# A gate stage with rows turned on VectorE, h added by accumulating loads and finished a pair later, and one row ring of four buffers

## The chip, the cores and the metric

The kernel runs on one core of a Trainium2 chip. The metric is the device time of one execution in microseconds (us), lower is better. The core has a matrix engine (TensorE, PE in the profile, with a separate row PEld for the loading of its weights), VectorE (DVE), ScalarE (ACT), GpSimd (POOL) and SyncE (SP). Each runs its own instructions in order; they wait for each other by semaphores. Transfers between the chip's memory (DRAM) and the on-chip buffers (SBUF) are issued by SP, ACT and POOL, each into a queue of its own, and run beside the engines. Matrix products go to banks of PSUM, which VectorE and ScalarE read.

## What is computed

One layer of a streaming encoder over 2048 prompt rows and 32 sample rows of width 1024, cut to what matters here:

```python
hn = rmsnorm(h, g_mix)
proj = hn @ w_in                                  # input projection, then two mixers -> yA, yB
h = h + concat([yA, yB], axis=-1) @ w_out         # "output stage"
gate = sigmoid(rmsnorm(h, g_ple) @ w_ple_gate)
h = h + (p @ w_ple) * gate                        # "embedding" p @ w_ple, then "gate stage"
y = rmsnorm(h, g_final)
```

Everything is float32; each operand of a product is split into a high and a low part, and three products (high-high, high-low, low-high) are added up.

## The kernel before, in words

**Tiles.** The 2048 rows are 16 tiles of 128, and the sample rows are a seventeenth tile of 32. From the output stage on, the tiles are taken in pairs (0 and 1, 2 and 3, ...). A pair is a 256x1024 by 1024x1024 product, which `seven` makes in seven products of quarters (Strassen-Winograd) in place of eight. With A11, A12 the upper tile's and A21, A22 the lower tile's halves, the kernel forms S1 = A21 + A22, S2 = S1 - A11, S3 = A11 - A21 and S4 = A12 - S2 on VectorE, and splits all of them; T1 to T4 are such sums of the weights. One quarter product is 12 matmuls of 128x128 by 128x512. They go to three banks X, Y, Z: X takes A11 W11, then adds S2 T2, then S3 T3, then A22 T4; between two of these, the state of X is read out by `carry` (parts kept for later: c_00, c_01 from X and c_11 from Z) or by `out` (a finished quarter). The next product into a bank therefore waits until the read before it is done. The order within a pair is X (A11 W11), Z (S1 T1), X (S2 T2), X (S3 T3), Y (A12 W21), Z (S4 W22), X (A22 T4); the tile scheduler orders instructions of neighbouring steps on each engine by what it reckons to be ready. A dictionary `between` gives work to be put at steps 1 to 6 between the products.

**Output stage** (about 559 to 722 us). `seven` runs for pairs o0 to o14, and the sample follows o12 (`ol`). x, the tile's input rows (128x1024), is loaded by `load_rows` on SP from a ring `xh` of 3 buffers. `h_ops` adds x to the products on VectorE: in `carry`, c_00 and c_01 read the first tile's x and c_11 the second's; in `out`, the finished h is written over x. `done_h` squares and sums the row on ScalarE (`sumsq`) and stores h to DRAM (`h_d`) on SP. `prep_h` loads the next pair's activations y on SP (ring `ya` of 5) and forms its sums. Beside this, one block of 128 gate weights per pair (two in places) is scaled: `scale_gate(k)` loads it on POOL's queue as two halves of 128x512 (gs) from a ring of its own, `qa`; after the next pair ScalarE scales both and stores them to `g_d` on its own queue. `next_gate` starts the scaling of the block before and the load of the next.

**Embedding** (722 to 762 us): p @ w_ple is made for most tiles and stored in `e_d`.

**Gate stage** (762 to 940 us): the sample goes first (`plain`), then pairs 0 to 12 in a loop, then `last_pair` (tiles 14 and 15). `prep_g(i + 2)` runs between the products of pair i and brings h of the next pair back from DRAM with the channel in the partition. For the pair's second tile, `turned_here` loads the rows in four blocks on SP and turns 32x32 blocks on VectorE. For the first tile, `turned` loads the rows (hn), ScalarE copies them in two halves (ho, in `qa`), and TensorE turns them by four transposes each into PSUM (pth). For the result, e and h of both tiles are loaded again on SP (`e` in `ya`, `h` in `xh`). `gate_ops` takes a quarter of the product: ScalarE applies the sigmoid, VectorE multiplies e by it and adds that to h. `done_g` then squares the row on ScalarE (`sumsq`, whose small root runs on POOL), multiplies by the root and g_final on VectorE, and stores the row on POOL's queue.

**What sets the order.** SP's transfers are issued in program order, and each waits for its buffer to come free, so one that waits holds up those behind it. POOL's queue carries the gate weights (output stage) and the finished rows (gate stage); ScalarE's queue carries the scaled gate weights. Buffers in a ring are handed out in turn, and a new user of a buffer waits for the last reader or writer of the former one.

Lines of the kernel before that matter: pools 1102, `h_ops` 1116 (VectorE's operations show as L1120), `done_h` 1143 (store at L1146), `scale_gate` 1162 (load L1170, scale L1174, store L1175), `load_rows` 324 (L327), the load of y at L314, `turned` with copy L1280 and transposes L1282, `turned_here` with L1293, `gate_ops` with L1310 to L1314, `done_g` L1318 (L1321, store L1322), `last_pair` with L1371 to L1401, and the products at L167.

Of the kernel before, what the change touches and what calls it, by code (L numbers as in the profile page):

```python
# [9 lines left out]
F32 = mybir.dt.float32  # L10
F32R = mybir.dt.float32r
AF = mybir.ActivationFunctionType
ALU = mybir.AluOpType
# [21 lines left out]
def trunk(ctx, tc, x_p, x_s, c_conv, c_pool, p_p, p_s, g_mix, w_in, conv_w, conv_b, pool_w,  # L35
# [271 lines left out]
    def ring4(t, name):  # L307
        return t.tile([P, D], F32, tag="t", name=name)
# [791 lines left out]

    with ExitStack() as s2:
        pool = lambda name, bufs: s2.enter_context(tc.tile_pool(name=name, bufs=bufs, reuse_waits="tile"))
        w3, qa, xh, st, ss, cmb = (pool(*a) for a in (
            ("w3", 1), ("qa", 2), ("xh", 3), ("st", 4), ("ss", 3), ("cmb", 8)))

        def quarters(name, W):
            c = halves(slot(f"{name}_c"))
# [54 lines left out]
        def scale_gate(k):  # L1162

            ts = [qa.tile([P, NH], F32, tag="q", name=f"gs_{k}_{half}") for half in range(2)]
            rows = w_gate.rearrange("(q k c) n -> k q c n", q=4, k=KC)[k]
            for half, t in enumerate(ts):
                nc.gpsimd.dma_start(t, rows[:, :, half * NH:half * NH + NH])  # L1170

            def rest():
                for half, t in enumerate(ts):
                    tc.keep_in_program_order(nc.scalar.activation(t, t, AF.Copy, scale=vec[:, 100 + k:101 + k]))  # L1174
                    nc.scalar.dma_start(g_d[k * P:k * P + P, half * NH:half * NH + NH], t)  # L1175

            return rest
# [94 lines left out]
        def turned(i):  # L1272

            r, n = tiles[i]
            t = load_rows(ya, "hn", i, h_d).rearrange("p (q k c) -> p k q c", q=4, k=KC)
            out = []
            for half in range(2):
                pt = tbank(f"pth_{i}_{half}")
                o = qa.tile([P, KH, P], F32, tag="q", name=f"ho_{i}_{half}")
                nc.scalar.copy(o[:n].rearrange("p k (q c) -> p k q c", q=4), t[:n, half * KH:half * KH + KH])  # L1280
                for k in range(KH):
                    nc.tensor.transpose(pt[:, k * P:k * P + n], o[:n, k], ident[:n, :n])  # L1282
                out.append(pt.rearrange("p (k t) -> p k t", k=KH))
            return out

        def turned_here(i):

            r, n = tiles[i]
            t = ring4(ya, f"hn_{i}")
            for q in range(4):  # L1290
                nc.sync.dma_start(t[q * 32:q * 32 + 32].rearrange("p (g c) -> p g c", g=4),
                                  h_d[r:r + P, q * 256:q * 256 + 256].rearrange("(g p) c -> p g c", p=32))
            nc.vector.transpose(t, t)  # L1293
            u = t.rearrange("p (g k t) -> p k g t", g=4, k=KC)
            return u[:, :KH], u[:, KH:]

        def gate_ops(h, e, n, name, i):
            scale = lambda at: rs_h[:n, i + at[0]:i + at[0] + 1]

            def carry(ps, at):  # L1300
                t = st.tile([P, NH], F32, tag="t", name=f"c_{name}_{at[0]}{at[1]}")
                nc.scalar.copy(t[:n], ps[:n])
                return t

            def out(ps, c, at):
                if c is None:
                    c = st.tile([P, NH], F32, tag="t", name=f"g_{name}_{at[0]}{at[1]}")
                    nc.scalar.activation(c[:n], ps[:n], AF.Sigmoid, scale=scale(at))
                else:
                    nc.vector.tensor_tensor(c[:n], ps[:n], c[:n], op=ALU.add)  # L1310
                    nc.scalar.activation(c[:n], c[:n], AF.Sigmoid, scale=scale(at))
                ee, hh = half_of(e, at, n), half_of(h, at, n)
                nc.vector.tensor_tensor(ee, ee, c[:n], op=ALU.mult)
                nc.vector.tensor_tensor(hh, hh, ee, op=ALU.add)  # L1314

            return carry, out

        def done_g(i, h):  # L1318
            r, n = tiles[i]
            rf = sumsq(h, n, f"f{i}")  # L1320
            nc.vector.scalar_tensor_tensor(h[:n], h[:n], rf[:n], g_bc[:n], op0=ALU.mult, op1=ALU.mult)  # L1321
            nc.gpsimd.dma_start(rows_of(y_p, y_s, r, n), h[:n])  # L1322

        def short_ops(h, e, n):
# [17 lines left out]
        def last_pair(i, A):  # L1342
# [1 line left out]

            pt = ring4(ya, "p_l")[:, :PLE]
            nc.sync.dma_start(pt, p_p[(i + 1) * P:(i + 2) * P])
            e = load_rows(ya, "e", i, e_d)
            wp = embedding_chunks("wl")  # L1350
            h = [load_rows(xh, "h", i + b, h_d) for b in range(2)]
            tt = nc.vector.tensor_tensor
            carry, _ = gate_ops(h, [e], P, f"g{i}", i)
            hg = [ring4(ya, f"hg_{b}") for b in range(2)]
            sums = [[], []]
            gate = {}

# [51 lines left out]
                finish(1, half, ps, m)  # L1409

            pps = embedded()
            seven(f"g{i}", A, W, carry, out, {5: lambda: second(1, NH)}, first_tile=True)
            second(0, NH // 2)

        def prep_g(i):

            A = {}
            whole = lambda t: t.rearrange("p k (g t) -> p k g t", g=4)

            def put(q, src, view=lambda t: t):  # L1420
                A[q] = cmb.tile([P, KH, 2, P], F32R, tag="c", name=f"g{i}_{q}")
                split(view(A[q][:, :, 0]), view(A[q][:, :, 1]), src)

            def comb(q, x, y, op, view=lambda t: t):
                t = ss.tile([P, KH, P], F32, tag="s", name=f"g{i}_f{q}")
                nc.vector.tensor_tensor(view(t), x, y, op=op)
                return t

            lower = []

            def first():
                lower.extend(turned_here(i + 1))

            def second():
                a21, a22 = lower
                s1 = comb("S1", a21, a22, ALU.add, whole)
                a11, a12 = turned(i)
                put("11", a11)
                s2 = comb("S2", s1, a11, ALU.subtract)
                s3 = comb("S3", whole(a11), a21, ALU.subtract, whole)  # L1440
                put("12", a12)
                put("S2", s2)
                s4 = comb("S4", a12, s2, ALU.subtract)
                put("S1", s1)
                put("S3", s3)
                put("S4", s4)
                put("22", a22, whole)

            S[i] = A
            return {2: first, 3: second}  # L1450
# [1 line left out]
        S = {}  # L1452
        n = tiles[NT - 1][1]
        A = short("gl", turned(NT - 1), n)
        for step in prep_g(0).values():
            step()
        for c in range(len(rest_e) - LATE, len(rest_e)):
            run(c)
        h, e = (load_rows(*a) for a in ((xh, "h", NT - 1, h_d), (ya, "e", NT - 1, e_d)))
        plain("gl", A, W, n, *short_ops(h, e, n))  # L1460
        done_g(NT - 1, h)
        for i in range(0, NT - 3, 2):
            A = S.pop(i)
            h = [load_rows(xh, "h", i + b, h_d) for b in range(2)]
            e = [load_rows(ya, "e", i + b, e_d) for b in range(2)]
            seven(f"g{i}", A, W, *gate_ops(h, e, P, f"g{i}", i), prep_g(i + 2))
            for b in range(2):
                done_g(i + b, h[b])
        last_pair(NT - 3, S[NT - 3])


# [27 lines left out]
```

## Time and profile before

| what | before |
|---|---|
| median of 3 runs | 944.54 us (944.16 to 944.74) |
| the profiled execution, its time and its span | 942.12 us, span 940.3 us |
| granted TensorE clock, mean | 0.994 |
| chain that ended last: PE's share | 74% |

The page of the profile gives each engine's busy time in us with its share of the span; PE and PEld overlap. Rows of the chain and of the timeline give start in us, length in us, engine, line and operation, the tile written and the tiles read, and a count; a square bracket at the end is how long the engine sat idle before it and on what. Rows of groups end with busy time and mean ns of one, then the idle time ahead and what ended it. Rows of transfers give the queue that issued them, how many there were, KB each and the median us from issue to landing. Names leave out the tile numbers.

### The profile page before, as it was taken

To read this page: it belongs to the slowest core of one execution; us is meant where nothing else is said; L and a number is where in the kernel's file an instruction comes from. 1 tells how busy PE (TensorE), PEld (TensorE's weight loads), DVE (VectorE), ACT (ScalarE), POOL (GpSimd) and SP (SyncE) were. 2 spreads that over 40 slices of the span, in tenths; PEclk is the share of its full clock that TensorE was granted. 3 is DMA by queue.
4 is the path that set the end of the run, shared out by engine and by line. 5 is a ranking of instruction groups with operands and counts; after the bars stand their busy time and mean duration, and the time that the engine had idled before them with its cause. 6 is when DMAs were issued, how large, how long until landed. Compare 5 with 4: busy or idle time off the path is not lost.

```text
span 940.3 us, 13055 instructions
## 1 busy us (share of the span) xinstructions
PE 920.7 (98%) x4599; PEld 831.5 (88%) x4599; DVE 726.3 (77%) x1230; ACT 480.5 (51%) x890; POOL 126.2 (13%) x244
## 2 busy tenths in 40 slices
PE   7999999999999999999999999999999999999996
PEld 5999999999999999999999987888878868888885
DVE  6697998899587978785777588765554797888985
ACT  5554555454444554443454356334334875555564
POOL 2101222120000110000000010211211001211113
PEclk8999999999999999999999999999999999999999
DMA  8336586696952655418655359865785883566653
GB/s 247 101 105 172 143 243 197 182 255 207 423 166 80 178 161 144 151 52 287 198 167 176 117 176 305 263 194 170 217 253 171 307 274 130 201 227 209 216 207 112
DMA packets 133214, 182.96 MB, mean 195 GB/s; under 512 B 11164, under 2 KB 105116, under 8 KB 131869
## 3 DMA queue, kind: packets, MB, share of 16 engines
q1 hardware_dynamic: 117165, 131.70, 45.2%
q0 software_dynamic: 13248, 44.93, 14.9%
q10 hardware_dynamic: 2736, 5.51, 1.8%
q8 instruction: 36, 0.59, 0.3%
q14 instruction: 29, 0.24, 0.1%
HBM read 127.23 MB, written 54.86 MB: 194 GB/s over the span
## 4 chain that ended last, share of the span: by engine, by line
PE 74%; DMA 3%; DVE 2%; ACT 2%; issue 0%; POOL 0%; POOLq 0%; DVEq 0%; ACTq 0%
PE x_o L167 9%; PE x_g L167 9%; PE e L102 5%; PE z_g L167 5%; PE x_zab L556 5%; PE z_o L167 4%; PE x_ch L556 4%; PE x_zbv L556 4%; PE z_zab L556 2%; PE y_g L167 2%; PE y_o L167 2%; PE b L556 2%; PE v L556 2%; PE zb L556 2%; PE za L556 2%; PE c L556 2%
## 5 line engine op out<-in xcount | busy, mean ns | idle before, releaser
L77 ACT CAST y_S<-y_fS 128x512 fp32r<-128x512 f32 x32 | 19.5, 621 | 42.5 <-PE x_o L167 18.9
L102 PE MATMUL e<-wq,pps 128*128 128x512 f32 (+1 forms) x156 | 38.8, 399 | 0.2 <-ACT pps L77 0.2
L406 DVE SCALAR_TENSOR_TENSOR xt<-xt,rstd_x,g_bc 128x1024 f32<-128x1024 f32 (+2 forms) x18 | 23.1, 1282 | 19.4 <-POOL rstd_x L73 18.0
L167 PE MATMUL x_g<-wg_b,g_S 128*128 128x512 f32 x128 | 35.9, 390 | 0.0
L167 PE MATMUL x_o<-wo_b,y_S 128*128 128x512 f32 x128 | 35.8, 391 | 0.0
L556 PE MATMUL z_ch<-B,w_ch_S 128*128 128x416 f32 x168 | 34.3, 352 | 0.9 <-ACT U L851 0.9
L556 PE MATMUL z_zab<-B,w_zab_S 128*128 128x416 f32 x168 | 34.1, 351 | 0.5 <-ACT U L851 0.5
L556 PE MATMUL x_zab<-B,w_zab_S 128*128 128x416 f32 x168 | 34.5, 352 | 0.1
L556 PE MATMUL z_zbv<-B,w_zbv_S 128*128 128x416 f32 x168 | 34.2, 352 | 0.0
L556 PE MATMUL x_zbv<-B,w_zbv_S 128*128 128x416 f32 x168 | 34.1, 351 | 0.0
L556 PE MATMUL x_ch<-B,w_ch_S 128*128 128x416 f32 x168 | 34.0, 351 | 0.0
L102 PEld LDWEIGHTS e<-wq,pps 128*128 128x128 f32 (+1 forms) x156 | 27.4, 182 | 6.9 <-ACT pps L77 0.5
L556 PEld LDWEIGHTS z_ch<-B,w_ch_S 128*128 128x128 f32 x168 | 31.2, 188 | 1.6 <-ACT U L851 1.2
L556 PEld LDWEIGHTS z_zab<-B,w_zab_S 128*128 128x128 f32 x168 | 31.3, 188 | 1.1 <-ACT U L851 0.8
L556 PEld LDWEIGHTS x_zab<-B,w_zab_S 128*128 128x128 f32 x168 | 31.2, 188 | 1.0 <-DVE w_zab_S L78 0.4
L556 PEld LDWEIGHTS x_ch<-B,w_ch_S 128*128 128x128 f32 x168 | 31.4, 188 | 0.3
L556 PEld LDWEIGHTS x_zbv<-B,w_zbv_S 128*128 128x128 f32 x168 | 31.3, 188 | 0.3
L556 PEld LDWEIGHTS z_zbv<-B,w_zbv_S 128*128 128x128 f32 x168 | 31.3, 188 | 0.4
L69 POOL TENSOR_SCALAR ms_f<-ssq_f 128x1 f32<-128x1 f32 (+1 forms) x15 | 8.8, 585 | 160.7 <-ACT junk L88 160.7
L77 ACT CAST y<-y 128x512 fp32r<-128x512 f32 x24 | 14.8, 618 | 29.4 <-PE x_o L167 13.8
L1321 DVE SCALAR_TENSOR_TENSOR h<-h,rstd_f,g_bc 128x1024 f32<-128x1024 f32 (+1 forms) x15 | 19.3, 1284 | 12.7 <-POOL rstd_f L73 12.7
L167 PEld LDWEIGHTS x_o<-wo_b,y_S 128*128 128x128 f32 x128 | 24.0, 188 | 5.0 <-ACT c_o L1125 0.3
(570 smaller groups left out, 2670.7 us busy)
## 6 DMA issues: line engine op xcount, KB each, us to landing
y<-y_d SPq DMA_DIRECT2D x16, 512.0 KB, 12.7
x<-in_x_prompt_dram SPq DMA_DIRECT2D x16, 512.0 KB, 9.7
h_d<-x SPq DMA_DIRECT2D x16, 512.0 KB, 4.5
h<-h_d SPq DMA_DIRECT2D x16, 512.0 KB, 3.6
xt<-in_x_prompt_dram SPq DMA_DIRECT2D x15, 512.0 KB, 12.7
e<-e_d SPq DMA_DIRECT2D x15, 512.0 KB, 5.9
out_dram<-h POOLq DMA_DIRECT2D x14, 512.0 KB, 3.0
p_dT<-T POOLq DMA_DIRECT2D x12, 512.0 KB, 6.2
```

Source lines behind the costliest of these rows:

```text
L69: nc.gpsimd.tensor_scalar(ms[:n], ssq[:n], scalar1=1.0 / D, scalar2=EPS, op0=ALU.mult, op1=ALU.add)
L77: ins = nc.scalar.copy(hi, src)
L102: nc.tensor.matmul(ps[:n], pps[:, a, k, :n], wp[k][b][:, cs], start=k + q == 0, stop=k == 1 and q == 2)
L167: nc.tensor.matmul(ps[:n], lhs[:, k, a, :n], w[b][:, k], start=start and k + q == 0, stop=k == KH - 1 and q == 2, skip_group_check=True)
L406: nc.vector.scalar_tensor_tensor(xt[:n], xt[:n], r[:n], g_bc[:n], op0=ALU.mult, op1=ALU.mult)
L556: nc.tensor.matmul(ps[:, :NB], lhs[:, k, x], b[:, k, y], start=start and k + q == 0, stop=stop and k == KH - 1 and q == 2, skip_group_chec ...
L1321: nc.vector.scalar_tensor_tensor(h[:n], h[:n], rf[:n], g_bc[:n], op0=ALU.mult, op1=ALU.mult)
```

## The change

Pools in the second half of the kernel: the ring `qa` is dropped and `xh` has four buffers of 128x1024 in place of three, in the same memory. Then:

- `scale_gate` takes one buffer of `xh` for a gate block; its halves are the halves of this buffer.
- `prep_g` turns both tiles of a pair on VectorE by `blocks` (four loads on SP into a buffer of `xh`) and `turned_here`; only the first pair (`here=False`) keeps `turned` for its first tile, whose copies ho now lie in a buffer of `xh`. The last pair's preparation goes by the new way too.
- In pairs 0 to 12, h is not loaded and not added on VectorE. After VectorE has multiplied a quarter of e by the gate, POOL issues an accumulating load that adds the 128x512 block of h from `h_d` to e in place. The sample and the last pair add h on VectorE as before.
- The rows of a pair are finished during the next pair: the squaring (`root_g`) at step 4, the multiplication and the store (`done_g`) at step 5, both kept in program order on their engine.
- `last_pair`: p_l moves to the ring `ss`, hg to `xh`, and the two rows of the pair before are finished at steps 4 and 5.

```diff
-        w3, qa, xh, st, ss, cmb = (pool(*a) for a in (
-            ("w3", 1), ("qa", 2), ("xh", 3), ("st", 4), ("ss", 3), ("cmb", 8)))
+        w3, xh, st, ss, cmb = (pool(*a) for a in (("w3", 1), ("xh", 4), ("st", 4), ("ss", 3), ("cmb", 8)))
...
-            ts = [qa.tile([P, NH], F32, tag="q", name=f"gs_{k}_{half}") for half in range(2)]
+            gs = ring4(xh, f"gs_{k}")
+            ts = [gs[:, half * NH:half * NH + NH] for half in range(2)]
...
+            both = ring4(xh, f"ho_{i}").rearrange("p (h k t) -> p h k t", h=2, k=KH)
             for half in range(2):
                 pt = tbank(f"pth_{i}_{half}")
-                o = qa.tile([P, KH, P], F32, tag="q", name=f"ho_{i}_{half}")
+                o = both[:, half]
...
-        def turned_here(i):
+        def blocks(i):
             r, n = tiles[i]
-            t = ring4(ya, f"hn_{i}")
+            t = ring4(xh if i > 1 else ya, f"hn_{i}")
             for q in range(4):
                 nc.sync.dma_start(t[q * 32:q * 32 + 32].rearrange("p (g c) -> p g c", g=4),
                                   h_d[r:r + P, q * 256:q * 256 + 256].rearrange("(g p) c -> p g c", p=32))
+            return t
+
+        def turned_here(t):
             nc.vector.transpose(t, t)
...
-                ee, hh = half_of(e, at, n), half_of(h, at, n)
+                ee = half_of(e, at, n)
                 nc.vector.tensor_tensor(ee, ee, c[:n], op=ALU.mult)
-                nc.vector.tensor_tensor(hh, hh, ee, op=ALU.add)
+                if h is None:
+                    r = tiles[i + at[0]][0]
+                    nc.gpsimd.dma_start(ee, h_d[r:r + P, at[1] * NH:at[1] * NH + NH], accum_op=ALU.add)
+                else:
+                    hh = half_of(h, at, n)
+                    nc.vector.tensor_tensor(hh, hh, ee, op=ALU.add)
...
-        def done_g(i, h):
+        def root_g(i, h, later=True):
+            return sumsq(h, tiles[i][1], f"f{i}", later=later)
+
+        def done_g(i, h, rf, later=True):
             r, n = tiles[i]
-            rf = sumsq(h, n, f"f{i}")
-            nc.vector.scalar_tensor_tensor(h[:n], h[:n], rf[:n], g_bc[:n], op0=ALU.mult, op1=ALU.mult)
+            ins = nc.vector.scalar_tensor_tensor(h[:n], h[:n], rf[:n], g_bc[:n], op0=ALU.mult, op1=ALU.mult)
+            if later:
+                tc.keep_in_program_order(ins)
             nc.gpsimd.dma_start(rows_of(y_p, y_s, r, n), h[:n])
...
-            pt = ring4(ya, "p_l")[:, :PLE]
+            pt = ss.tile([P, NH], F32, tag="s", name="p_l")[:, :PLE]
...
-            hg = [ring4(ya, f"hg_{b}") for b in range(2)]
+            hg = [ring4(xh, f"hg_{b}") for b in range(2)]
...
-            seven(f"g{i}", A, W, carry, out, {5: lambda: second(1, NH)}, first_tile=True)
+            seven(f"g{i}", A, W, carry, out, {4: roots, 5: lambda: (finished(), second(1, NH))}, first_tile=True)
...
-        def prep_g(i):
+        def prep_g(i, here=True):
...
+            rows = [blocks(i + b) for b in range(1 - here, 2)]
+            ready = []
 
             def first():
-                lower.extend(turned_here(i + 1))
+                ready.extend(turned_here(rows[0]))
 
             def second():
-                a21, a22 = lower
-                s1 = comb("S1", a21, a22, ALU.add, whole)
-                a11, a12 = turned(i)
-                put("11", a11)
+                if here:
+                    a11, a12 = ready
+                    put("11", a11, whole)
+                    a21, a22 = turned_here(rows[1])
+                    s1 = comb("S1", a21, a22, ALU.add, whole)
+                else:
+                    a21, a22 = ready
+                    s1 = comb("S1", a21, a22, ALU.add, whole)
+                    a11, a12 = map(whole, turned(i))
+                    put("11", a11, whole)
...
-        done_g(NT - 1, h)
+        done_g(NT - 1, h, root_g(NT - 1, h, False), False)
+        ready = []
+
+        def roots():
+            for x in ready:
+                x.append(root_g(*x))
+
+        def finished():
+            while ready:
+                done_g(*ready.pop(0))
+
         for i in range(0, NT - 3, 2):
             A = S.pop(i)
-            h = [load_rows(xh, "h", i + b, h_d) for b in range(2)]
+            steps = prep_g(i + 2)
             e = [load_rows(ya, "e", i + b, e_d) for b in range(2)]
-            seven(f"g{i}", A, W, *gate_ops(h, e, P, f"g{i}", i), prep_g(i + 2))
-            for b in range(2):
-                done_g(i + b, h[b])
+            seven(f"g{i}", A, W, *gate_ops(None, e, P, f"g{i}", i), {**steps, 4: roots, 5: finished})
+            ready.extend([i + b, e[b]] for b in range(2))
         last_pair(NT - 3, S[NT - 3])
```

11 lines of the change are left out of this document (5 added, 6 removed).

## The prediction

> **What bounds the kernel now.** I read the engine shares first, then the clock and the chain that ended last, then who made TensorE wait in the two stages that the diff touches, then a table of one pair in each stage.
>
> ```profile
> PE 920.7 (98%) x4599; PEld 831.5 (88%) x4599; DVE 726.3 (77%) x1230; ACT 480.5 (51%) x890; POOL 126.2 (13%) x244
> PEclk8999999999999999999999999999999999999999
> PE 74%; DMA 3%; DVE 2%; ACT 2%; issue 0%; POOL 0%; POOLq 0%; DVEq 0%; ACTq 0%
> ...
> PE y_o L162 <- ACT wo_c L1191: 0.5, 1, 0.5
> ...
> 596.60 5.44 PE x_o L167 x24
> 615.85 5.44 PE x_o L167 x24
> ...
> 618.41:637.62 19.21, 19.21 (x85) 15.69 (x84) 11.78 (x18) 7.67 (x14) 3.58 (x7) 1.00 0.77 219
> 787.80:807.75 19.95, 19.95 (x93) 16.57 (x93) 17.65 (x27) 11.70 (x21) 3.49 (x6) 1.00 0.43 143
> 887.54:907.69 20.15, 20.15 (x95) 16.76 (x95) 17.67 (x27) 11.49 (x21) 3.36 (x6) 1.00 0.66 236
> ```
>
> TensorE is busy for 98% of the span at full clock, and from 550 us on its longest wait is 0.5 us. The chain shows 24 products in 5.44 us, so one takes 0.227, and consecutive output pairs start their first product 19.25 us apart (596.60 and 615.85 are the same place in two pairs). The window rows (length, then busy time of PE, PEld, DVE, ACT, POOL, clock, DMA share, GB/s) show an output pair of 19.2 us and a gate pair of 19.95 to 20.15, both with PE busy throughout; DVE is at 61% in the one and 88% in the other. So a PE instruction removed is time gained, and any other change costs only if it makes PE wait, which it hardly does now.
>
> **The gate stage: transposes leave TensorE.** This is what the diff takes away in seven pairs.
>
> ```profile
> 824.84 1.03 PE L1282 MATMUL pth<-ident,ho 128*128 128x128 f32 x8
> 825.63 2.10 PE L167 MATMUL z_g<-wg_d,g_S 128*128 128x512 f32 x8
> ...
> L1314 DVE TENSOR_TENSOR h<-h,e 128x512 f32<-128x512 f32 x28 | 18.6, 684 | 0.2
> L1293 DVE STREAM_TRANSPOSE hn<-hn 128x1024 f32<-128x1024 f32 x8 | 9.9, 1237 | 0.0
> ...
> h<-h_d SPq DMA_DIRECT2D x16, 512.0 KB, 3.6
> out_dram<-h POOLq DMA_DIRECT2D x14, 512.0 KB, 3.0
> ```
>
> Eight transposes stand between two stretches of products and advance PE by 825.63 - 824.84 = 0.79 us (their 272 ns each overlap). Without them in pairs two to eight: -7 x 0.79 = -5.5 us. DVE takes over 1.24 us a pair (one more transpose) and sheds four h additions, 4 x 0.684 = 2.74, so its 17.65 becomes about 16.15 in a PE pair of 19.95 - 0.79 = 19.16: still 3 us of slack, so I price DVE's part at nothing; if DVE did set the pair, it would have to grow past 19.16. ScalarE loses its two copies ahead of the transposes.
>
> h now comes by four accumulating loads a pair, issued on POOL behind the multiplications. Nothing here shows such a load. Plain 512 KB moves take 3.0 and 3.6 us, and in the crowded output stage 256 KB by POOL's queue took 9.3 (row below). The last multiplication of a pair falls some 4.5 us into the next pair by its place in DVE's order; in ScalarE's new order the squaring of the rows stands behind the copy of the next pair's fourth product, 48 x 0.227 + 0.6 = 11.5 us in. Between them lie 7 us. With 3 to 4 us the load is hidden; with 9.3, ScalarE's squaring waits 2.3 us, and behind it in order stand the sigmoids and casts of the products in flight. I take hidden, nearest to the moves between the same buffers, and keep 2 us a pair (14 in all) as the upper end, the price of a rival; below nothing there is no gain, since PE has no wait here to lose. Eight short SyncE loads a pair for the turned rows replace four and three 512 KB loads; the DMA share of 0.43 to 0.66 in the two windows leaves room, price 0.
>
> **The tail.** Finishing rows a pair later puts rows 12 and 13 behind the last pair's fifth product.
>
> ```profile
> 917.26 1.29 DVE L1321 SCALAR_TENSOR_TENSOR h<-h,rstd_f,g_bc 128x1024 f32<-128x1024 f32 x1 [0.73 <-POOL rstd_f L73]
> 921.05 1.28 DVE L1321 SCALAR_TENSOR_TENSOR h<-h,rstd_f,g_bc 128x1024 f32<-128x1024 f32 x1 [0.45 <-POOL rstd_f L73]
> ...
> 929.09 0.68 DVE L1371 TENSOR_TENSOR c_g<-e_l,c_g 128x512 f32<-128x512 f32 x1
> 930.67 0.68 DVE L1372 TENSOR_TENSOR h<-h,c_g 128x512 f32<-128x512 f32 x1
> 932.77 0.75 DVE L1371 TENSOR_TENSOR g_l<-e_l,g_l 128x256 f32<-128x256 f32 x2 [1.42 <-ACT g_l L1401]
> ```
>
> Today these two 1.29 us operations run at 917 and 921, where DVE has gaps. In the new order both stand ahead of the operation now at 929.09, on DVE, in the last 10 us. Of their 2.57 us, the 1.42 us that DVE waits before 932.77 absorb a part: +1.2 us (2.57 - 1.42, rounded up), between 0 and 2.6.
>
> **The output stage: the row ring.** The diff gives the gate's rows (gs) one whole buffer in the ring that held only x. Four buffers in place of three, but now three users per pair, x of both tiles and gs. Following the allocations: x_4 takes x_2's buffer, x_5 that of gs_1, x_6 x_4's, x_7 that of gs_2, x_8 x_6's, x_9 x_7's, x_10 x_8's, x_11 that of gs_4, x_12 x_10's, x_13 that of gs_5. So the first x of a pair waits until the first x of the pair before is stored, and the second until gs is scaled and stored. Before, the first x was loaded a whole pair ahead.
>
> ```profile
> 597.35 0.33 SPq L1146 DMA_DIRECT2D h_d<-x  x1
> ...
> 605.40 0.33 SPq L327 DMA_DIRECT2D x<-in_x_prompt_dram  x1
> ...
> 618.41 2.88 PE L167 MATMUL x_o<-wo_c,y 128*128 128x512 f32 x12
> 619.33 0.32 SPq L1146 DMA_DIRECT2D h_d<-x  x1
> 619.52 0.33 ACTq L1175 DMA_DIRECT2D g_d<-gs  x1
> 619.74 0.46 SPq L327 DMA_DIRECT2D x<-in_x_prompt_dram  x1
> 621.33 0.69 DVE L1120 TENSOR_TENSOR c_o<-x_o,x 128x512 f32<-128x512 f32 x1 [2.03 <-PE x_o L167]
> 622.08 0.50 PE L167 MATMUL x_o<-wo_a,y_S 128*128 128x512 f32 x1
> 622.65 0.37 SPq L314 DMA_DIRECT2D y<-y_d  x1
> 623.55 0.33 SPq L327 DMA_DIRECT2D x<-in_x_prompt_dram  x1
> 625.22 0.75 POOL L1170 DMA_DIRECT2D gs<-in_w_ple_gate_dram  x1 [1.58 <-DMA g_d<-gs]
> 627.13 0.69 DVE L1120 TENSOR_TENSOR c_o<-z_o,x 128x512 f32<-128x512 f32 x1
> ...
> L1120 DVE TENSOR_TENSOR c_o<-z_o,x 128x512 f32<-128x512 f32 x5 | 3.4, 686 | 1.0 <-DMA x<-in_x_prompt_dram 1.0
> ...
> h_d<-x SPq DMA_DIRECT2D x13, 512.0 KB, 4.9
> x<-in_x_prompt_dram SPq DMA_DIRECT2D x12, 512.0 KB, 9.7
> gs<-in_w_ple_gate_dram POOLq DMA_DIRECT2D x12, 256.0 KB, 9.3
> ...
> DMA to landing us min/median/max: 9.2/9.2/9.2
> ...
> DMA to landing us min/median/max: 10.3/10.3/10.3
> ...
> DMA to landing us min/median/max: 7.6/7.6/7.6
> ```
>
> Call E the start of a pair's own products (618.41). Today the x loaded at 605.40 (9.2 us to landing by the first of the last three rows; 623.55 took 10.3, its like a pair on 7.6) serves the sum at 621.33, and the one issued at 619.74 = E+1.3 serves the sum at 627.13 = E+8.7. Over five pairs that second sum waited 1.0 us in all for its load, so the load issued at E+1.3 takes up to 7.4 us (627.13 - 619.74).
>
> *First x.* After the change it is the load issued at about E+1.3, behind the last h store in SyncE's order. Its landing time L is bounded by 3.6 us (the 512 KB row above) and 7.4; I take 6.5, towards the row with the same neighbours. The first sum ends at E+1.3+6.5+0.7 = E+8.5. The next product (S2) needs the bank that this sum frees. In the instruction order that the changed program is built with, PE has 32 to 34 products ahead of S2 where it now has 16 (622.08 is E+3.7): it is covered to 32 x 0.227 = E+7.3 or 34 x 0.227 = E+7.7. Stall 0.8 to 1.2 us a pair; 0 at L = 5, 2.1 at 7.4.
>
> *Second x.* It waits in SyncE's queue for the store of gs. The POOL row at 625.22 shows when the second gs store of this burst had landed, E+6.8 at the latest; I take issue at E+6.3, behind a y load on the same queue and beside the gs loads on POOL's. The loads that end today's burst are the nearest: 9.2 and 10.3, or 7.6 where less is under way. With 9.0 it lands at D = E+15.3. Then come the sum c_o<-z_o and, in DVE's new order, five operations to the one that frees the bank of the last product, 6 x 0.69 + 0.1 = 4.2, and that product's 12 x 0.227 = 2.7: the pair ends at D+6.9 = E+22.2 against E+19.25, so +3.0 us. That is for the pairs of tiles 4, 6 and 10. Pair 8 (x_9 in x_7's buffer, free with an h store of 4.9 us) and pair 12 (the y load beside it is the 32-row sample's) I give L near 7 and D = E+12.8 (0.9 + 4.9 + 7): there the end by this load alone would be E+19.7, so the first stall decides, at its upper 1.2 each, since h stores slip with the stalls before them.
>
> Sum of the output stage: 3 x 3.0 + 2 x 1.2 = +11.4 us. With the first load at 3.6 and the second at 6 nothing stalls (0); with the second at 10.4 everywhere it is 5 x 4.4 = 22. The pair of tile 2, the sample and the pair of tile 14 keep their loads far enough ahead: 0.
>
> [...]
>
> **Sum.** -5.5 + 1.2 + 11.4 = +7.1 us. The profiled execution took 942.12 us (span 940.3 and 1.8 around it), 2.4 under the median of the runs; the difference is put on the median: 944.54 + 7.1 = 951.6.
>
> **Rivals.**
> 1. *Only the first x is late.* If the second x's load takes about 6 us, it lands by E+12.3 and the pair ends in time; the five first stalls at their lower 0.8 remain. 944.54 - 5.5 + 1.2 + 4.0 = 944.2, no change that can be told. For it: h stores of 4.9 and the plain 3.6. Against: 9.2 and 10.3 at this very place.
> 2. *The reordered products hide both loads* (the other side): the first x lands within 5 us and the second within 6, as PE's cover has doubled. 944.54 - 5.5 + 1.2 = 940.2. Against: the 1.0 us that the second sum waits today, with a load issued at the same moment.
> 3. *The gate stage gets a wait of its own*, from the accumulating loads: at 9.3 us each, the squaring on ScalarE waits 2.3 us a pair with the casts behind it, of which 0.8 to 2 reach PE: 7 times that on top of the forecast, 957 to 965.6. For it: 9.3 on POOL's queue. Against: the 7 us between, and a DMA share of 0.43 to 0.66.
> 4. *DVE becomes the bound of the gate pairs*, so that the turned transposes bring nothing: no -5.5, 944.54 + 1.2 + 11.4 = 957.1. Against: 16.15 of 19.16 by the rows. [...]
>
> **Chances.** Forecast 0.60, rival 1 0.16, rival 2 0.10, rivals 3 and 4 together 0.14. Runs of this kernel tell about 0.2% (1.9 us, 942.65 to 946.4) from no change. Rival 1 lies mostly within it (0.12 same, 0.04 faster), rival 2 is faster (0.10), and of the forecast's lower end 0.04 is same: faster 0.14, same 0.16, slower 0.70. Most of the chance lies above; the likeliest case's own range is 946 (five first stalls of 1.2 alone) to 959. The range asked for leaves out rival 2 and the upper part of rivals 3 and 4: 941.5 to 960.
>
> **What would show it.** In the changed profile: no PE transposes in gate pairs two to eight and pairs of about 19.2 us; PE waits for DVE c_o (S2, then the last two products) in the pairs of tiles 4 to 12, behind DVE waits for the DMA of x; gaps in PE's row between 600 and 700 us and a stage about 11 us longer; ScalarE's squaring in the gate stage waiting for nothing; the two late row operations after 925 and an end about 1.2 us further behind the last product. The prediction is wrong if the output pairs stay at 19.25 us (loads hidden), or if PE waits in the gate stage.

## The result, and the profile after

The changed kernel takes 949.8 us (median of 5 runs, 948.78 to 953.19) against 944.46 for the kernel before (5 runs): ratio 1.0062, 95% interval 1.0043 to 1.0082, so slower by 5.3 us. The forecast was 951.6, the range 941.5 to 960. The profiled execution of the changed kernel is the slowest of its five: 953.19 us, span 951.4.

The page of the changed kernel (busy time per engine; granted clock in 40 slices), then who made TensorE wait from 570 us on (us in all, times, longest):

```profile
PE 918.9 (97%) x4543; PEld 825.9 (87%) x4543; DVE 716.7 (75%) x1209; ACT 472.9 (50%) x876; POOL 144.8 (15%) x272
...
PEclk8999999999999999999999999999999999999998
```

```profile
PE x_o L167 <- DVE c_o L1119: 6.7, 6, 1.9
PE x_g L167 <- ACT c_g L1307: 1.8, 1, 1.8
PE y_o L162 <- ACT wo_c L1191: 0.5, 1, 0.5
```

PE has 56 instructions fewer, the eight transposes of seven pairs. It was never held for more than 0.5 us in this part of the kernel before. Now it waits six times in the output stage for VectorE's sum c_o, once per pair from o4 to o14, and once in the last pair for ScalarE.

To split the difference by stage, four marks are enough: the last product of pair o0, that of o14, the first product of the gate's pair 0, and the last pair's first Y product. Timeline rows, first of the kernel before, then of the changed one (start, length, engine, line, operation, count):

```profile
577.38 2.88 PE L167 MATMUL x_o<-wo_T,y 128*128 128x512 f32 x12
719.22 2.89 PE L167 MATMUL x_o<-wo_T,y 128*128 128x512 f32 x12
770.40 2.90 PE L167 MATMUL x_g<-wg_c,g 128*128 128x512 f32 x12
913.00 0.39 PE L167 MATMUL y_g<-wg_c,g 128*128 128x512 f32 x1
```

```profile
579.52 2.88 PE L167 MATMUL x_o<-wo_T,y 128*128 128x512 f32 x12
731.42 2.89 PE L167 MATMUL x_o<-wo_T,y 128*128 128x512 f32 x12
782.84 2.92 PE L167 MATMUL x_g<-wg_c,g 128*128 128x512 f32 x12
919.38 0.39 PE L167 MATMUL y_g<-wg_c,g 128*128 128x512 f32 x1
```

| stretch | before | after | difference | forecast |
|---|---|---|---|---|
| ahead of the first mark | 577.4 | 579.5 | +2.1 | 0 |
| output stage, o0 to o14 | 141.8 | 151.9 | +10.1 | +11.4 |
| seam (embedding) | 51.2 | 51.4 | +0.2 | 0 |
| gate pairs | 142.6 | 136.5 | -6.1 | -5.5 |
| tail, to the end of the span | 27.3 | 32.0 | +4.7 | +1.2 |

The five differences add up, within rounding, to the 11.1 us between the two spans. That is more than the 5.3 of the medians: the execution before was 2.3 us below its median, the one after 3.4 above. The first row is work that the change does not touch (an experiment below shows its scatter), and part of the second is a clock loss in one pair (0.72 over 6 us of o6), which experiments 1 and 3 do not have.

**Output stage.** Pair o6 in the changed kernel (E, the start of its own products, is 622.65):

```profile
622.65 2.43 PE L167 MATMUL x_o<-wo_c,y 128*128 128x512 f32 x10
...
624.69 0.33 SPq L327 DMA_DIRECT2D x<-in_x_prompt_dram  x1
...
630.24 0.33 SPq L327 DMA_DIRECT2D x<-in_x_prompt_dram  x1
...
631.19 0.69 DVE L1119 TENSOR_TENSOR c_o<-x_o,x 128x512 f32<-128x512 f32 x1 [2.00 <-DMA x<-in_x_prompt_dram]
...
631.93 0.50 PE L167 MATMUL x_o<-wo_a,y_S 128*128 128x512 f32 x1 [1.87 <-DVE c_o L1119]
...
637.18 0.68 DVE L1119 TENSOR_TENSOR c_o<-z_o,x 128x512 f32<-128x512 f32 x1
```

The first x is issued at E+2.0, right behind the h store, and lands 6.5 us later; VectorE waits 2.00 us for it and PE 1.87 for VectorE. The second x is issued at 630.24, after its gs store, and the sum that needs it at 637.18 does not wait for it (in two other pairs, o4 and o10, it does). The two windows below (length, busy PE, PEld, DVE, ACT, POOL, clock, DMA share, GB/s) show what comes after the stall:

```profile
610.00:616.00 6.00, 5.56 (x24) 4.37 (x25) 2.37 (x4) 1.14 (x2) 0.00 (x0) 1.00 0.63 183
631.00:637.00 6.00, 5.07 (x15) 4.03 (x16) 2.41 (x4) 0.43 (x1) 1.07 (x2) 0.72 0.70 210
```

After the stall of 1.27 us in pair o4 the granted clock stayed at 1.00 and PE made 24 products in 5.56 us of busy time; after that of 1.87 us in o6 it was 0.72 and PE made 15 in 5.07 us. Pair o6 is 3.88 us longer than its like before: 1.87 waiting, and of the other 2.0 all but about 0.3 are slower products (experiments 1 and 3, at a clock of 1.00, show 0.3 beyond the stall of this pair too).

**Gate stage.** Two pairs of the changed kernel, the squaring of rows, and the accumulating loads:

```profile
820.96:840.00 19.04, 19.04 (x86) 15.77 (x84) 17.09 (x25) 10.55 (x18) 6.63 (x11) 1.00 0.85 221
840.00:859.04 19.04, 19.04 (x86) 15.77 (x84) 17.61 (x24) 10.56 (x18) 6.23 (x11) 1.00 1.00 237
...
L88 ACT ACTIVATE junk<-e 128x1024 bf16<-128x1024 f32 x14 | 14.8, 1059 | 1.0 <-DMA e<-h_d 0.5
...
e<-h_d POOLq DMA_DIRECT2D x28, 256.0 KB, 6.8
```

A pair takes 19.04 us in place of 19.95, PE busy throughout. The accumulating loads land in 6.8 us (median), twice what the forecast took, and still ScalarE waited for them only once in 14 rows, for 0.5 us. VectorE is at 17.1 and 17.6 of 19.04 in these two pairs, the busiest; over the five pairs from 801.92 to 897.18 us its mean is 16.5. That is close, but not the bound. The DMA share is 0.85 and 1.00 here, where the kernel before had 0.43 to 0.66, and PE still does not wait.

**Tail.** The last pair of the changed kernel:

```profile
915.30 0.58 POOL L1336 DMA_DIRECT2D out_dram<-e  x1 [0.29 <-DVE e L1333]
...
919.74 1.70 SPq L1239 DMA_DIRECT2D wlr<-in_w_ple_dram  x2
...
925.46 1.05 ACT L77 CAST wl<-wlr 128x1024 fp32r<-128x1024 f32 x1 [5.29 <-DMA wlr<-in_w_ple_dram]
...
929.46 1.19 PE L167 MATMUL x_g<-wg_b,g_S 128*128 128x512 f32 x4 [1.75 <-ACT c_g L1307]
```

The raw embedding weights (wlr) of the last tile come in buffers of `ya` that rows 10 and 11 still hold, since rows are now finished a pair later. Their load waits for the store of row 10, ScalarE waits 5.29 us for the load, and behind that cast stands the copy (c_g) that PE needs.

### The profile page after: what moved, and what is told of

Its sections match the earlier page's. It is cut to its first block, busy times and chain, and to the rows that moved or that the text cites. A ratio compares the mean times of both kernels' runs of the same rounds, so it can differ in the third digit from the quotient of the medians.

```text
span 951.4 us, 12975 instructions
## 1 busy us (share of the span) xinstructions
PE 918.9 (97%) x4543; PEld 825.9 (87%) x4543; DVE 716.7 (75%) x1209; ACT 472.9 (50%) x876; POOL 144.8 (15%) x272
## 5 line engine op out<-in xcount | busy, mean ns | idle before, releaser
L77 ACT CAST y_S<-y_fS 128x512 fp32r<-128x512 f32 x32 | 19.4, 621 | 62.6 <-PE x_o L167 47.8
L1321 POOL DMA_DIRECT2D e<-h_d x28 | 24.9, 909 | 53.3 <-DVE e L1318 53.2
L556 PEld LDWEIGHTS z_ch<-B,w_ch_S 128*128 128x128 f32 x168 | 31.2, 188 | 1.8 <-ACT U L851 1.4
L556 PEld LDWEIGHTS x_zab<-B,w_zab_S 128*128 128x128 f32 x168 | 31.2, 188 | 1.4 <-DVE w_zab_S L78 0.8
L167 PEld LDWEIGHTS x_g<-wg_b,g_S 128*128 128x128 f32 x128 | 23.9, 188 | 7.1 <-ACT c_g L1307 2.2
L167 PE MATMUL x_o<-wo_a,y_S 128*128 128x512 f32 x64 | 22.9, 421 | 6.7 <-DVE c_o L1119 6.7
```

Source lines behind the costliest of these rows:

```text
L77: ins = nc.scalar.copy(hi, src)
L167: nc.tensor.matmul(ps[:n], lhs[:, k, a, :n], w[b][:, k], start=start and k + q == 0, stop=k == KH - 1 and q == 2, skip_group_check=True)
L556: nc.tensor.matmul(ps[:, :NB], lhs[:, k, x], b[:, k, y], start=start and k + q == 0, stop=stop and k == KH - 1 and q == 2, skip_group_chec ...
L1321: nc.gpsimd.dma_start(ee, h_d[r:r + P, at[1] * NH:at[1] * NH + NH], accum_op=ALU.add)
```

## The experiments

**1. The ring alone.** The kernel before with the shared ring of four and nothing else of the change.

```diff
-        w3, qa, xh, st, ss, cmb = (pool(*a) for a in (
-            ("w3", 1), ("qa", 2), ("xh", 3), ("st", 4), ("ss", 3), ("cmb", 8)))
+        w3, xh, st, ss, cmb = (pool(*a) for a in (("w3", 1), ("xh", 4), ("st", 4), ("ss", 3), ("cmb", 8)))
...
-            ts = [qa.tile([P, NH], F32, tag="q", name=f"gs_{k}_{half}") for half in range(2)]
+            gs = ring4(xh, f"gs_{k}")
+            ts = [gs[:, half * NH:half * NH + NH] for half in range(2)]
...
+            both = ring4(xh, f"ho_{i}").rearrange("p (h k t) -> p h k t", h=2, k=KH)
...
-                o = qa.tile([P, KH, P], F32, tag="q", name=f"ho_{i}_{half}")
+                o = both[:, half]
```

> The kernel before with one part of the change alone: ring of four, the gate block's rows (gs) and the copies ahead of TensorE's transposes (ho) in it; the gate stage keeps TensorE's transposes, h loads and additions. Theory (the shared ring makes the first x of a pair late): the stretch from the first pair's last product to the last pair's (T4 of o0 to T4 of o14) grows from 141.8 us to about 152, as in the changed kernel (151.9); PE waits about 6 to 7 us for DVE c_o; time about 954. Rival (the output stage's loss belongs to the one profiled execution or to the rest of the change): within 2 us of the kernel before, no PE wait on c_o.

952.33 us, ratio 1.0098 (1.0074 to 1.0121). The output stretch is 148.4 us, 6.5 longer; gate pairs stay at 19.95 and the tail at 27.8. Who made PE wait, and the two sums that read x (groups of VectorE; after the second bar the idle time ahead and what ended it):

```profile
PE x_o L167 <- DVE c_o L1119: 4.8, 6, 1.3
```

```profile
L1119 DVE TENSOR_TENSOR c_o<-x_o,x 128x512 f32<-128x512 f32 x14 | 9.7, 690 | 19.0 <-PE x_o L167 12.1 <-DMA x<-in_x_prompt_dram 6.9
L1119 DVE TENSOR_TENSOR c_o<-z_o,x 128x512 f32<-128x512 f32 x7 | 4.8, 681 | 0.0
```

The sums of the first x waited 6.9 us for loads and held PE 4.8 us; those of the second x waited nothing at all. So the ring costs the output stage 6.5 us, through the first x alone. By the medians the kernel is 9.5 us slower than before; the stretches account for 7.4 of it, and its first mark comes 2.7 us later. The stretch is 3.5 us shorter than in the changed kernel's profile: the stalls add up to 4.8 us in place of 6.7, none exceeds 1.3 us, and the clock stayed at 1.00. Of the 6.5, the wait rows name 4.8; the rest, about 0.3 us a pair, has no row, and I leave it open.

**2. Rings apart, two ways.** The changed kernel with gs in two halves of its own and x in three buffers, the ring of four opened behind the output stage (first block), and the same with the last pair's buffers dealt out anew (second block).

```diff
-        w3, xh, st, ss, cmb = (pool(*a) for a in (("w3", 1), ("xh", 4), ("st", 4), ("ss", 3), ("cmb", 8)))
+        w3, st, ss, cmb = (pool(*a) for a in (("w3", 1), ("st", 4), ("ss", 3), ("cmb", 8)))
+        s_o = s2.enter_context(ExitStack())
+        qa, xh = (s_o.enter_context(tc.tile_pool(name=name, bufs=bufs, reuse_waits="tile")) for name, bufs in (("qa", 2), ("xo", 3)))
...
+        s_o.close()
+        xh = pool("xh", 4)
         W = sums_slots("wg")
```

> The changed kernel, but in the output stage gs has its two halves and x its three buffers as before; the ring of four is opened after that stage. Theory: output stretch back to 141.8 us, gate pairs at 19.05 us; 10 us less than the changed kernel, so 940 to 943. Rival (part of the loss is in the gate stage, in late accumulating loads or a full VectorE): output stretch back, but time still 946 or more.

951.1 us, ratio 1.0086 (1.0065 to 1.0106): a miss for the time, not for the stage. The rival's 946 or more came, but not for its reason. The output stretch was back at 142.0, with no wait on c_o. But the seam grew from 51.2 to 56.0, and the first gate pair from 19.96 to 21.18, since eight of the sample's products now fall into it. The two together are 6.0 us longer than before. PE waits in that seam, and the first load of gate weights:

```profile
PE x_gl L270 <- DVE gl L78: 3.6, 1, 3.6
...
735.28 0.37 SPq L1271 DMA_DIRECT2D wg_r<-g_d  x1
```

The load stands 13.9 us behind the last output product of that run (721.40); in the kernel before, the second such load stood 4.1 behind (723.29 against 719.22), and one had gone out ahead. Loads that used to start while the output stage ran now wait for the stage to end. Of the 6.0 us, 3.6 are PE's wait; the four products behind it (768.30) took 1.97 us, where the kernel before took 1.07 for them, and the page has the granted clock at 8 tenths in this slice (758 to 782 us), at 9 in those beside it. The boundary cost about what the ring had in experiment 1, 6.5.

```diff
-            wp = embedding_chunks("wl")
-            h = [load_rows(xh, "h", i + b, h_d) for b in range(2)]
-            hg = [ring4(xh, f"hg_{b}") for b in range(2)]
+            wp = embedding_chunks("wl", xh)
+            h = [load_rows((xh, ya)[b], "h", i + b, h_d) for b in range(2)]
+            hg = [ring4((xh, ya)[b], f"hg_{b}") for b in range(2)]
```

> Both edits, own rings in the output stage and the last pair's buffers dealt out anew. If the two losses are separate and add up: about 13 us below the changed kernel, 936.5 to 939.5, faster than the kernel before by 5 to 8 us. Rival: a wait moves elsewhere and it stays above 941.

948.16 us, ratio 1.0046 (1.003 to 1.0062): it stayed above 941, for the same seam (56.2). The tail fell to 29.9.

**3. The tail alone.** The second block of the last experiment on the changed kernel.

> The changed kernel, only the last pair's buffers dealt out anew: raw embedding weights (wlr) and h of tile 14 and hg of tile 14 from the row ring, h of tile 15 and hg of tile 15 from ya, so that the wlr loads do not wait for the stores of rows 10 and 11. Theory (the tail's extra 4.7 us come from ScalarE waiting 5.3 us for wlr): from the last pair's first Y product to the end about 28.5 us in place of 32.0; time 946 to 947. Rival (it is the two late row operations themselves that cost the tail): 31 to 32 us, time 949 to 950.

948.79 us, ratio 1.0064 (1.0042 to 1.0086). The tail is 29.9 us in place of 32.0; ScalarE no longer waits for wlr. So 2.1 of the 4.7 us were that load and 2.6 the rest, the late row operations among it. The expectation of 28.5 was missed, and so was that for the time, which hardly moved (1.0064 against 1.0062; the two intervals, each 0.4% wide, cannot tell 2 us either way). The profiled execution also shows a transpose that waited 2.91 us for its rows, with the wlr loads issued right behind them, and a gate pair of 20.09 us there. The output stretch repeats the ring's price, 148.6, again with no wait of the second sum for its load.

**4. Old pools, new gate stage.** gs and ho in halves of their own as before, the row ring of three for the turned rows too, nothing opened anew, last pair as above.

> The changed gate stage with the pools of the kernel before (gs and ho in two halves of their own, row ring of three, never opened anew) and the last pair's buffers dealt out anew. The variant that opened the ring of four after the output stage lost 6 us at the seam, because the gate weights' loads waited for the whole ring. Theory (output loss is the shared ring alone, gate pairs gain 0.9 us each, tail costs 2.6): output stretch 141.8 us, seam 51.2 as before, gate stretch 136.5, tail 29.9; 3 to 4 us faster than the kernel before. Rival (three buffers are too few for two turned tiles a pair): gate pairs above 19.3 us, no gain.

945.98 us, ratio 1.0035 (1.0018 to 1.0053). Output stretch 141.9 and seam 51.2, as before: with its own buffers the stage loses nothing. But the gate stretch was 139.4 in place of 136.5, with four pairs of 19.4 to 20.8 us, and three transposes of VectorE waited for their rows:

```profile
845.88 1.25 DVE L1297 STREAM_TRANSPOSE hn<-hn 128x1024 f32<-128x1024 f32 x1 [2.13 <-DMA hn<-h_d]
...
864.08 1.25 DVE L1297 STREAM_TRANSPOSE hn<-hn 128x1024 f32<-128x1024 f32 x1 [2.89 <-DMA hn<-h_d]
...
884.15 1.25 DVE L1297 STREAM_TRANSPOSE hn<-hn 128x1024 f32<-128x1024 f32 x1 [4.68 <-DMA hn<-h_d]
```

The rival held for the pairs: with three buffers the stage keeps 3.2 of the 6.1 us that it had won, and experiment 8, which gives it the fourth buffer back in place of the two halves, brings 2.1 more. The time is 2.3 us above the kernel before, which these stretches do not explain: they add up to 0.7 us less than before. The profiled execution reaches the first mark 3.0 us later, and what this is experiment 7 takes up. The output stage needs gs kept apart.

**5. Two x buffers.** As experiment 2's first edit, with ("xo", 2).

> The changed kernel with gs in two halves of its own and only two buffers for x in the output stage (the ring of four opened after it, so the seam costs its 5 to 6 us here too). The first x of a pair is then as late as in the changed kernel, but the second waits for an h store only and not for gs. Theory (the first x carries the output stage's loss): PE waits on c_o of 4 to 7 us, output stretch 147.5 to 149. Rival, the term sum of the prediction (the second x, late behind gs, carries 9 of 11.4 us): stretch below 145.

965.44 us, ratio 1.024 (1.0213 to 1.0267); output stretch 155.2. Neither expectation: both sums waited. PE waited 8.0 us for the products into X, 7.2 of them for the first sum, and the second sum waited 1.1 to 2.9 us in all seven pairs from o2 on. The run does not part the two x, since with two buffers the second x is late as well; experiment 1 does. It adds one thing: a stall of 1.94 us was followed by a clock of 0.72, one of 1.87 us was not.

```profile
613.00:619.00 6.00, 5.82 (x18) 4.48 (x19) 2.11 (x4) 1.14 (x2) 0.00 (x0) 0.72 0.75 157
636.00:642.00 6.00, 5.67 (x24) 4.49 (x25) 2.25 (x4) 1.14 (x2) 0.02 (x1) 1.00 0.72 173
```

**6. Turning alone.** Both tiles turned on VectorE, h loaded and added there as before, rows finished in their own pair; hg of the last pair comes from `ya`, as before.

```diff
-            hg = [ring4(xh, f"hg_{b}") for b in range(2)]
+            hg = [ring4(ya, f"hg_{b}") for b in range(2)]
...
-            seven(f"g{i}", A, W, carry, out, {4: roots, 5: lambda: (finished(), second(1, NH))}, first_tile=True)
+            seven(f"g{i}", A, W, carry, out, {5: lambda: second(1, NH)}, first_tile=True)
...
+            h = [load_rows(xh, "h", i + b, h_d) for b in range(2)]
...
-            seven(f"g{i}", A, W, *gate_ops(None, e, P, f"g{i}", i), {**steps, 4: roots, 5: finished})
-            ready.extend([i + b, e[b]] for b in range(2))
+            seven(f"g{i}", A, W, *gate_ops(h, e, P, f"g{i}", i), steps)
+            for b in range(2):
+                done_g(i + b, h[b], root_g(i + b, h[b], False), False)
```

> The changed kernel with one part of its gate stage alone: both tiles of a pair turned on VectorE, but h loaded on SP and added on VectorE and rows finished in their own pair, as before (row ring of four kept, so the output stage keeps its loss). Theory A (VectorE has slack, the accumulating loads only free it): DVE about 18.9 us busy in gate pairs of 19.05 to 19.2. Theory B (rival 4: without the accumulating loads VectorE sets the pair): pairs of 19.6 us or more with PE waiting for DVE.

954.09 us, ratio 1.0104 (1.007 to 1.0138). Two gate pairs of this run, and a timeline row of SP's queue:

```profile
819.21:838.25 19.04, 19.04 (x85) 15.77 (x84) 16.84 (x25) 10.60 (x19) 3.79 (x6) 1.00 0.63 199
838.25:858.22 19.97, 19.37 (x85) 15.63 (x84) 18.27 (x27) 10.54 (x19) 3.51 (x6) 1.00 0.72 239
...
846.99 5.10 SPq L1292 DMA_DIRECT2D hn<-h_d  x8
```

The first three pairs run at 19.04 to 19.08 us with all additions still on VectorE, so the turning is what shortens a pair. From the fourth on they take 19.4 to 20.2: the loads of turned rows go out in one burst 8.7 us into the pair, and PE waits up to 0.6 us for ScalarE's cast behind VectorE. The first three do fewer operations on VectorE (23 to 26) than a later pair (27 in three of the four), so they do not show that it would hold. Turning alone keeps about 2.6 of the 6.1 us: the gate stretch is 140.0 us. Theory B comes nearer from the fourth pair on, though VectorE is not full (18.3 of 19.97); the wait rows name only 1.1 us of the loss. That the two h buffers of the ring hold the burst back, so that the accumulating loads would give buffers more than VectorE time, I read from the order of the loads; it was not tried with more buffers.

**7. The kernel before, once more.**

> The kernel before, unchanged, for a second profile. In the first profile the output stage began (first product with wo) at 559.6 us, in eight profiles of changed kernels at 559.2 to 563.7, most near 562, though nothing ahead of that point is changed. If that spread is chance, this one lies in it too and the ratio is 1; if the changed kernels really start the stage later, it is at 559 to 560 again. The stages behind it should repeat within 0.2 us: 141.8, 51.2, 142.6 and 27.3.

942.64 us, ratio 1.0 (0.9985 to 1.0016). The first output product of pair o0 began at 561.1 us in place of 559.6, inside the spread of the changed kernels (559.2 to 563.7); the stretches were 142.1, 51.6, 143.1 and 27.3. So the 2.1 us ahead of the first mark are within what this unchanged work shows from run to run, and single stretches repeat within 0.5 us, not the 0.2 expected. Since experiments 1 and 4 are 2 to 3 us slower by their medians than their stretches tell, a slightly later start of some changed kernels is not ruled out.

**8. The losses taken out.** gs keeps one buffer of 128x1024 of its own (`xg`), x a ring of three; in the gate stage `xg` holds the lower tile of every second pair, so turned rows have four buffers again. Memory as before, no ring opened late, last pair as in experiment 3.

```diff
-        w3, xh, st, ss, cmb = (pool(*a) for a in (("w3", 1), ("xh", 4), ("st", 4), ("ss", 3), ("cmb", 8)))
+        w3, xg, xh, st, ss, cmb = (pool(*a) for a in (
+            ("w3", 1), ("xg", 1), ("xh", 3), ("st", 4), ("ss", 3), ("cmb", 8)))
...
-            gs = ring4(xh, f"gs_{k}")
+            gs = ring4(xg, f"gs_{k}")
...
-            both = ring4(xh, f"ho_{i}").rearrange("p (h k t) -> p h k t", h=2, k=KH)
+            both = ring4(xg, f"ho_{i}").rearrange("p (h k t) -> p h k t", h=2, k=KH)
...
-            t = ring4(xh if i > 1 else ya, f"hn_{i}")
+            t = ring4(ya if i < 2 else xg if i % 4 == 3 else xh, f"hn_{i}")
```

> The changed gate stage; gs has one buffer of 128x1024 of its own and x a ring of three; in the gate stage that same buffer takes the blocks of every second pair's lower tile, so that turned tiles again have four buffers, and nothing is opened anew; last pair dealt out anew. Theory (losses are the shared ring, then too few gate buffers, then the tail): output stretch 141.8, seam 51.2, gate 136.5 to 137.5, tail 29.9: 3 to 4 us faster than the kernel before. Rival (ring of three was not what slowed the gate pairs, but loads queued behind others on SP): gate 139 or more, no gain.

938.46 us (936.33 to 939.21), ratio 0.9956 (0.9939 to 0.9973): 4.2 us faster than the kernel before (942.7 on the same chip) and about 10 faster than the changed one by their ratios (1.0062 to 0.9956). Its marks and waits:

```profile
577.19 1.07 PE L167 MATMUL x_o<-wo_T,y 128*128 128x512 f32 x4
719.08 2.89 PE L167 MATMUL x_o<-wo_T,y 128*128 128x512 f32 x12
...
770.26 1.09 PE L167 MATMUL x_g<-wg_c,g 128*128 128x512 f32 x4
...
907.55 0.39 PE L167 MATMUL y_g<-wg_c,g 128*128 128x512 f32 x1
```

```profile
PE x_g L167 <- DVE c_g L1316: 0.5, 1, 0.5
```

The stretches are 141.9, 51.2, 137.3 and 29.9 us (span 937.4): the ring's loss is gone, 5.3 of the gate's gain is kept, the tail still costs 2.6. The expectations held, the time by a little more than expected. A transpose still waits 2.16 us for its rows (at 842.73), but PE waits only once in the gate stage, 0.5 us, behind it.

**9. Row 13 last.** The same, with the last two rows finished apart.

```diff
-            seven(f"g{i}", A, W, carry, out, {4: roots, 5: lambda: (finished(), second(1, NH))}, first_tile=True)
+            seven(f"g{i}", A, W, carry, out, {4: roots, 5: lambda: (finished(1), second(1, NH))}, first_tile=True)
             second(0, NH // 2)
+            finished()
...
-        def finished():
-            while ready:
+        def finished(n=2):
+            while ready and n:
                 done_g(*ready.pop(0))
+                n -= 1
```

> The same, but row 13 is finished after the last tile's own work in place of ahead of it. Theory (VectorE's two late row operations lengthen the tail): tail about 1 us shorter than in that kernel. Rival (its store then ends last): no shorter, or longer.

940.32 us, ratio 0.9979 (0.9965 to 0.9992); tail 31.2, not shorter but 1.3 longer. The row's store is now issued behind the last tile's own, which goes out at 932.09 and used to end the kernel. The first line is that store in experiment 8, the other two are of this run:

```profile
932.93 0.37 ACTq L1407 DMA_DIRECT2D out_dram<-hg  x1
...
932.09 0.37 ACTq L1407 DMA_DIRECT2D out_dram<-hg  x1
933.32 0.63 POOL L1337 DMA_DIRECT2D out_dram<-e  x1 [2.01 <-DVE e L1334]
```

The rival held: the row's own store then ends last. Half of the theory held too: counted from the last pair's first Y product (907.55 in experiment 8, 908.09 here), the last tile's own store goes out 24.0 us later in place of 25.4, so one late row operation did hold it back, by 1.4 us.

## Why the prediction came out, point by point

- *What bounds the kernel* held: PE was the engine to watch, and the stages' differences are PE's waits and PE's removed work.
- *Gate, -5.5*: measured -6.1, pairs of 19.04 against the 19.16 that the forecast gave. Taking VectorE's extra transpose and fewer additions as free was right (16.5 us of 19.04 busy over five pairs, 16.15 forecast), and so was the rejection of the rival in which VectorE sets the pair. It is right for the whole change only: without the accumulating loads and the late finish (experiment 6) pairs from the fourth on are back at 19.4 to 20.2.
- *Accumulating loads hidden*: right, with the price mis-sized. They take 6.8 us, not 3 to 4; the forecast's 7 us between the last multiplication and the squaring (8.2 us in the pair that begins at 840.00) covered them with little to spare. The price of nothing for the short loads held too, though the DMA share rose to 1.00.
- *First x*: right in place and size. Issue E+1.3 forecast, E+2.0 found in o6; landing 6.5 and 6.5; stall 0.8 to 1.2 forecast, 0.5 to 1.9 found. The pair of tile 14 was wrongly left out: it stalled 1.10 us.
- *Second x, +3.0 in three pairs*: this term failed. The step that failed is the choice of 9.0 us for its landing, by the nearest loads of the old burst. In the changed kernel's o6 it takes at most 6.9 us (630.24 to 637.18), and the sum waits 0 in experiments 1 and 3. A likely reason, not shown, is that the gs loads that crowded the old burst now wait for an h store themselves:

```profile
630.64 0.74 POOL L1170 DMA_DIRECT2D gs<-in_w_ple_gate_dram  x1 [4.86 <-DMA h_d<-x]
...
613.75 0.61 PE L167 MATMUL x_o<-wo_c,y 128*128 128x512 f32 x2
616.06 0.69 DVE L1119 TENSOR_TENSOR c_o<-z_o,x 128x512 f32<-128x512 f32 x1 [1.87 <-DMA x<-in_x_prompt_dram]
```

  The first of these rows is 0.4 us after the second x was issued, where before one half of gs went out 2.2 us ahead of the last x load of the burst. In the changed kernel's profile the second sum did wait, 3.4 us in all (1.87 in o4, the last row, and 1.48 in o10), and still no loss is to be seen. Pair o4 is 2.00 us longer than before, 0.7 beyond its stall of 1.27; but in experiments 1 and 3, where its second sum waits for nothing, it is 0.8 and 0.7 beyond its stall as well. Two of o6's products, 0.45 us, now run inside o4 (the second row). Rival 1, only the first x late, was the right mechanism.
- *Sum of the stage, +11.4*: 10.1 in the profiled execution and 6.5 to 6.7 where the ring is the same (experiments 1 and 3). The 9 us put on the second x were not there; in the profiled execution a lower clock in o6 (0.72), longer first stalls and the pair of tile 14 made up for most of them. The sum was near for partly the wrong reason, and that is luck.
- *Tail, +1.2 (0 to 2.6)*: 4.7. Without the wait for wlr it is 2.6 (experiment 3), the upper bound that the forecast gave the two late row operations; experiment 9 shows 1.4 for one of them. The step missed is another one, worth 2.1: the forecast followed the row ring's users but not those of `ya`, where e is now held a pair longer and the last tile's weights come next.
- *The sum*: +7.1 forecast, +5.3 by the medians. The stages add up to this only with the ring's price of experiments 1 and 3 (6.6 - 6.1 + 4.7 + 0.2 = 5.4). The second x was 9 too dear and the tail 3.5 too cheap: the direction was understood, that the number came so near is partly luck.

## What to carry to other kernels

When a ring gets one more buffer and one more kind of user, count its users per round: four buffers for three a round were worse here than three for two (by 6.5 us of the output stage in experiment 1), since a load that went out a pair ahead then went out a store and a landing before its use. Follow every ring whose buffers are held longer, to the last round, where other tiles come into it. A loss in one stage can hide a gain in another: by stage, this change won 6 us, and once gs had its own buffer and the last pair's buffers were dealt out anew the kernel was 0.4% faster than before.

## What the runs showed of the hardware

In three places a short stall of TensorE cost about twice its length. After stalls of 1.87, 1.94 and 2.60 us (the changed kernel, experiments 5 and 6) the granted clock over the next 6 us was 0.72 and the pair grew by 2.0 to 2.3 us beyond the stall. About 1.6 us of that goes with the clock, since the same pairs of experiment 1, at a clock of 1.00, grew by 0.3 (o6) and 0.8 (o4) beyond theirs. After stalls of 1.27 and 1.75 us in the changed kernel and another of 1.87 us in experiment 5 it stayed at 1.00. After the one of 3.58 us in the seam of experiment 2, four products took 1.97 us in place of the 1.07 of the kernel before. No run shows what parts these stalls: two of 1.87 us ended differently, the one in o6 of the changed kernel at 0.72, the one in experiment 5 at 1.00.
